# Shift and scale of two channel tiles by VectorE products along a channel's weights, and h by ScalarE

## The chip, the cores and the metric

The kernel runs on one core of one Trainium2 chip. The core has five engines, each with a queue of its own that is worked off in order: TensorE (PE in the profile, its weight loads PEld), VectorE (DVE), ScalarE (ACT), GpSimd (POOL) and SyncE (SP), which issues most of the DMA transfers. SBUF is the memory on the chip, with 128 partitions; PSUM holds what TensorE accumulates. The metric is the device time in microseconds (us) of one execution.

## What is computed

One layer of a backbone with two streams of 256 tokens each, context and latent, 2048 channels wide. Only this part of the reference is touched by the change:

```python
sc = jax.nn.silu(c)
scc = jax.nn.silu(c_ctx)
shift, scale, gate = jnp.split(sc @ w_ada[l] + b_ada[l], 3, axis=-1)
shift_c, scale_c, gate_c = jnp.split(scc @ w_ada[l] + b_ada[l], 3, axis=-1)
hc = _rmsnorm(ctx, g_pre[l]) * (1.0 + scale_c) + shift_c
zc = hc @ (w_in[l][:, :XBC_W + DT_W] if last else w_in[l])
hx = _rmsnorm(x, g_pre[l]) * (1.0 + scale[:, None]) + shift[:, None]
zx = hx @ w_in[l]
```

`_rmsnorm(x, g)` is x times 1/rms of its token, times g. After this follow a convolution, a bidirectional state-space scan, a spatial gating unit, an output projection and a last norm.

## The kernel before

The channels are cut into 16 tiles of 128, one channel on each partition, and the 512 tokens (context first, then latent) lie along the free dimension: `xT[:, k, :]` is channel tile k. h = x/rms * ha + hb is made tile by tile, where ha and hb are one number for each channel and stream. Products with `w_in` run in float32 split into two parts: a high part, rounded, and the low rest, so that each tile of outputs takes three matmuls (`mm3`: high by high, high by low, low by high). `hhi` and `hlo` are the two parts of h, `hi_st` and `lo_st` those of a weight row.

**The first stage** (to about 133.9 us) does three things at once.

1. *1/rms* (lines 260 to 282). Each of the 16 tiles is squared, by ScalarE and VectorE in turn, and summed over the partitions by matmuls with ones into `pss`. A transpose, a matmul with `sel` (`psb`), a square root, a reciprocal and another transpose give `rb`, 1/rms of each token on all partitions. A few warm-up matmuls (`warm`) lie in between.
2. *ha and hb* (`ada_mm`, `ada_fin`). The weights `w_ada` for shift and scale come in 32 chunks of 1 MB, two for each channel tile. Channel tiles 0 and 1 are a unit by themselves, the others form units of two: (2,3), (4,5) up to (14,15). A chunk of a pair holds a quarter of the input channels for its unit; `ada_mm` multiplies it by silu(c) and silu(c_ctx) (`sc`) on TensorE, 16 matmuls in float32, shown as 32 records, into `psada`. When a unit is complete, `ada_fin` transposes it on VectorE, and ScalarE makes ha and hb with two small activations for each tile.
3. *The rows* (line 372 on). Row kt takes weight row kt (`wst`, 480 KB, split by `split_st`: a cast on ScalarE, a small and a large subtraction on VectorE) and tile kt of h (`make_h`), and adds its share to `psdt` and to seven output tiles `psx`, two of which take latent tokens alone and are half as long. In `make_h`, VectorE multiplies x by ha and by rb, ScalarE adds hb and rounds (`hhi`), and VectorE takes the rest (`hlo`), each for the two streams apart.

The order on TensorE, VectorE, ScalarE and GpSimd is written by hand (`manual_schedule`): what `row_steps` lists for a row is issued in that order. ("m", i) stands for the products of output tile i (-1 is `psdt`), ("a", ci) for chunk ci, ("f", u) for `ada_fin`, ("h", k) for `make_h`, ("s", k) for `split_st`. From row 5 on a row is, in order, the split for the next row, two chunks, in odd rows the end of a unit, h for the next row, and its own eight products:

```python
return nxt[1:] + a + f + nxt[:1] + m
```

SyncE issues the loads in the order of the program: x in four transfers, then chunks and weight rows as line 372 on has them. A load waits until its buffer is free; there are six buffers for chunks (`raw0`) and three for weight rows (`st3`).

The last row (15) has an order of its own, `LAST`: `psdt`, tiles 4 and 5, each followed by a copy out of PSUM by VectorE (`zq`), then `dt_tok`, then the rest. `dt_tok` copies `psdt` by ScalarE and turns it by four matmuls against `fold` (`pstok`). `fold` is a small matrix made from the identity at line 165, at the start.

**The later stages** hold the convolution, the scan, the latent projections and the output projection. They have an order by hand up to the latent projections, and draw 121 weight tiles of 1 MB through four buffers that take the place of the first stage's. Later, `gate_tile` (line 884) forms the gate by another way than `ada_mm`: VectorE multiplies 2048 weights of a channel by c, laid out along the free dimension, and sums them in the same instruction (`accum_out`).

## Time and profile before

| | us |
|---|---|
| median of 3 runs | 995.4 (995.04 to 996.1) |
| the profiled execution | 995.27 |
| its span, first to last instruction | 993.6 |
| mean granted TensorE clock | 0.995 |

The profile is of one execution. Its page gives busy times of each engine and groups of instructions; other views of the same trace are the chain of work that ended last (followed back from the last instruction to what released each step), the timeline, the groups of a stretch, and a table of busy times by stretch.

How the page's slices and queues look:

```profile
PE   8999999999999999999999999999999999999996
PEld 3788887778787878787888888887888888888885
DVE  4345478877877665665667766666555554445636
ACT  4233348566656554545445434454565563346522
POOL 0000002423443221224000000000000000000000
PEclk9999999999999999999999999999999999999998
DMA  9999744233314324135888777774455445556722
```

Each digit is the busy share of one fortieth of the span (24.8 us) in tenths. The first stage fills a little over five of them: TensorE is near full there, VectorE at about a half, and the DMA engines are full for four slices. A group of instructions reads, for example, "L884 DVE SCALAR_TENSOR_TENSOR junk<-gate,cb 128x2048 bf16<-128x2048 f32 x16 | busy, mean ns of one | idle of the engine before them, and who released it": line, engine, operation, output and inputs, shape, count. Matmuls are pipelined: one has started its successor before its own modelled end, so the distance of two starts tells more than a duration.

### The profile page before, as it was taken

The page shows a single profiled execution, that of the slowest core. Times are in us where ns is not written, and L with a number is a line of the kernel's source. Part 1 is how long each engine was busy: PE and PEld are TensorE (multiplying, and loading weights), DVE is VectorE, ACT ScalarE, POOL GpSimd, SP SyncE. Part 2 cuts the span into 40 slices and gives each one's busy share as a digit, 9 for nine tenths or more (in the row PEclk, how much of TensorE's full clock was granted, in tenths as well). Part 3 has the DMA queues.
Part 4 walks back from the last instruction along what each step waited for, and adds up shares of the span by engine and source line. Part 5 has one row for each costly group of instructions (what it writes and reads, how often), then busy time and mean ns, then how long its engine had stood idle before and what let it go on. Part 6 is the DMA issues. An engine that isn't in the chain of part 4 may idle for free.

```text
span 993.6 us, 14183 instructions
## 1 busy us (share of the span) xinstructions
PE 976.9 (98%) x5636; PEld 791.0 (80%) x5636; DVE 622.6 (63%) x944; ACT 494.0 (50%) x759; POOL 112.3 (11%) x162
## 2 busy tenths in 40 slices
PE   8999999999999999999999999999999999999996
PEld 3788887778787878787888888887888888888885
DVE  4345478877877665665667766666555554445636
ACT  4233348566656554545445434454565563346522
POOL 0000002423443221224000000000000000000000
PEclk9999999999999999999999999999999999999998
DMA  9999744233314324135888777774455445556722
GB/s 379 419 417 419 300 179 170 85 128 128 128 43 170 127 85 158 54 138 203 301 306 294 280 263 291 266 284 171 170 173 204 174 169 212 181 200 235 274 85 84
DMA packets 31554, 207.28 MB, mean 209 GB/s; under 512 B 4080, under 2 KB 4208, under 8 KB 7808
## 3 DMA queue, kind: packets, MB, share of 16 engines
q1 hardware_dynamic: 28656, 192.52, 51.8%
q0 software_dynamic: 2112, 12.65, 3.7%
q10 hardware_dynamic: 720, 1.20, 0.3%
q8 instruction: 44, 0.72, 0.3%
q14 instruction: 22, 0.18, 0.1%
HBM read 204.20 MB, written 2.16 MB: 208 GB/s over the span
## 4 chain that ended last, share of the span: by engine, by line
PE 73%; issue 10%; DMA 9%; DVE 5%; ACT 1%; POOL 1%; SPq 0%; DVEq 0%; POOLq 0%; ACTq 0%
PE psx L138 10%; PE psx L140 10%; PE psx L139 10%; PE pa L1026 5%; PE pa L1028 5%; PE pa L1027 5%; DMA gate<-in_wada_dram 5%; PE pm L1075 3%; PE pm L1074 3%; PE pm L1073 3%; PE psada L215 3%; PE pq L1074 2%; PE pq L1075 2%; PE pq L1073 2%; DVE lo_w L82 2%
## 5 line engine op out<-in xcount | busy, mean ns | idle before, releaser
L82 DVE TENSOR_TENSOR lo_w<-w,hi_w 128x1024 fp32r<-128x1024 f32 x173 | 210.5, 1223 | 146.0 <-ACT hi_w L81 146.0
L81 ACT CAST hi_w<-w 128x1024 fp32r<-128x1024 f32 x173 | 182.0, 1052 | 202.3 <-PE pa L1028 130.4
L1026 PE MATMUL pa<-hi_w,hhi 128*128 128x512 f32 x512 | 202.4, 395 | 0.0
L1028 PE MATMUL pa<-hi_w,hlo 128*128 128x512 f32 x512 | 199.5, 390 | 0.0
L1027 PE MATMUL pa<-lo_w,hhi 128*128 128x512 f32 x512 | 199.3, 389 | 0.0
L138 PE MATMUL psx<-hhi,hi_w 128*128 128x512 f32 (+1 forms) x400 | 153.6, 384 | 0.0
L140 PE MATMUL psx<-hhi,lo_w 128*128 128x512 f32 (+1 forms) x400 | 145.9, 365 | 0.0
L139 PE MATMUL psx<-hlo,hi_w 128*128 128x512 f32 (+1 forms) x400 | 145.7, 364 | 0.0
L1026 PEld LDWEIGHTS pa<-hi_w,hhi 128*128 128x128 f32 x512 | 96.2, 188 | 20.6 <-issue 1.6
L1028 PEld LDWEIGHTS pa<-hi_w,hlo 128*128 128x128 f32 x512 | 96.1, 188 | 20.2
L1027 PEld LDWEIGHTS pa<-lo_w,hhi 128*128 128x128 f32 x512 | 96.2, 188 | 19.5 <-issue 0.2
L495 DVE SCALAR_TENSOR_TENSOR xbc<-psx,pc,xbc 128x248 f32<-128x248 f32 (+1 forms) x204 | 83.5, 472 | 34.1 <-ACT xbc L479 33.1
L420 DVE TENSOR_TENSOR lo_w<-w,hi_w 128x1024 fp32r<-128x1024 f32 x61 | 79.4, 1308 | 23.8 <-ACT hi_w L414 23.7
L138 PEld LDWEIGHTS psx<-hhi,hi_w 128*128 128x128 f32 x400 | 75.5, 189 | 13.4 <-issue 3.1
L140 PEld LDWEIGHTS psx<-hhi,lo_w 128*128 128x128 f32 x400 | 75.4, 189 | 12.6
L139 PEld LDWEIGHTS psx<-hlo,hi_w 128*128 128x128 f32 x400 | 75.6, 189 | 12.1 <-issue 1.7
L414 ACT CAST hi_w<-w 128x1024 fp32r<-128x1024 f32 x61 | 63.5, 1044 | 26.0 <-PE psx L139 12.9
L884 DVE SCALAR_TENSOR_TENSOR junk<-gate,cb 128x2048 bf16<-128x2048 f32 x16 | 36.6, 2290 | 22.8 <-DMA gate<-in_wada_dram 22.8
L1073 PE MATMUL pm<-hi_w,hhi 128*128 128x512 f32 x128 | 50.0, 390 | 0.0
L1074 PE MATMUL pm<-lo_w,hhi 128*128 128x512 f32 x128 | 49.9, 390 | 0.0
L1075 PE MATMUL pm<-hi_w,hlo 128*128 128x512 f32 x128 | 49.6, 389 | 0.0
L138 PE MATMUL psx<-hhi,hi_st 128*128 128x512 f32 (+1 forms) x112 | 41.3, 368 | 0.0
(219 smaller groups left out, 1324.3 us busy)
## 6 DMA issues: line engine op xcount, KB each, us to landing
w<-in_wlat_dram SPq DMA_DIRECT2D x64, 1024.0 KB, 4.8
ada<-in_wada_dram SPq DMA_DIRECT2D x32, 1024.0 KB, 14.7
w<-in_wout_dram SPq DMA_DIRECT2D x32, 1024.0 KB, 4.8
w<-in_wxbc_dram SPq DMA_DIRECT2D x25, 1024.0 KB, 4.8
gate<-in_wada_dram SPq DMA_DIRECT2D x16, 1024.0 KB, 5.8
R<-acs POOLq DMA_DIRECT2D x8, 1024.0 KB, 5.1
wst<-in_wst_dram SPq DMA_DIRECT2D x16, 480.0 KB, 14.9
xT<-in_xch_dram SPq DMA_DIRECT2D x4, 1024.0 KB, 8.0
```

The lines of the kernel that those rows point to most:

```text
L81: nc.scalar.copy(hi, raw)
L82: nc.vector.tensor_tensor(lo, raw, hi.bitcast(F32), op=ALU.subtract)
L138: nc.tensor.matmul(ps, lhsT=whi, rhs=hhi[k][:, s], start=start, stop=False)
L139: nc.tensor.matmul(ps, lhsT=whi, rhs=hlo[k][:, s], start=False, stop=False)
L140: nc.tensor.matmul(ps, lhsT=wlo, rhs=hhi[k][:, s], start=False, stop=stop)
L495: nc.vector.scalar_tensor_tensor(ao, zi, cw[:, k : k + 1], ao, op0=ALU.mult, op1=ALU.add)
L1026: nc.tensor.matmul(pa[tk], lhsT=hhi[k][:, t], rhs=whi[:, w], start=k == 0, stop=False)
L1027: nc.tensor.matmul(pa[tk], lhsT=hhi[k][:, t], rhs=wlo[:, w], start=False, stop=False)
L1028: nc.tensor.matmul(pa[tk], lhsT=hlo[k][:, t], rhs=whi[:, w], start=False, stop=k == KT - 1)
L1073: nc.tensor.matmul(p, lhsT=yh[:, t], rhs=whi[:, w], start=j == 0, stop=False)
L1074: nc.tensor.matmul(p, lhsT=yh[:, t], rhs=wlo[:, w], start=False, stop=False)
L1075: nc.tensor.matmul(p, lhsT=yl[:, t], rhs=whi[:, w], start=False, stop=hf == 0 and j == 15)
```

## The change

- **Tiles 12 and 13** no longer go through `ada_mm`. Their four chunks are laid out with 2048 weights of one output channel along the free dimension, one chunk for scale and one for shift of each tile, and `ada_v` multiplies such a chunk by silu(c) of one stream, laid out the same way on all partitions, and sums it, on VectorE. Two chunks and two streams make four products for a tile (`v12.0.0` to `v12.1.1`, `v13.0.0` to `v13.1.1`), eight in all. `ada_vfin` (step "e") then makes ha and hb as before. The unit (12,13) is gone.
- **silu(c) on all partitions** is made at the start: `c_diag` (VectorE) puts four times 128 values on diagonals, `c_rows` (TensorE) multiplies them by ones, `c_keep` (ScalarE) copies the result into `y`, which is free in the first stage. There are eight such blocks of 512. The warm-up matmuls fall from eight to three.
- **1/rms in front**: VectorE multiplies all of x by `rb` tile by tile (`norm`): tile 0 within the split of row 0, tiles 1 to 3 ahead of row 0, and tiles 4 to 15 in one block in row 0 (step "n").
- **h by ScalarE**: an activation with ha as scale and hb as bias makes h. For tiles 0 to 3 it writes `hhi` directly, and VectorE makes the unrounded h a second time for `hlo`. From tile 4 on it writes h in place for each stream, a copy rounds it, and VectorE takes the rest in one operation of 512 in place of two of 256.
- **The order**: the rows follow a table `WITH`, the loads a table `LOADS`. `load_more` issues loads in that order as far as buffers are free: four chunk buffers at first, since two of the six hold the squares and diagonals, and six after `make_h(0)`. Chunks that stood in pairs stand partly apart ("p3 a6.0 p2 a6.1 p3": three products, a chunk, two products, a chunk, three products).
- **`fold`** is made in `dt_tok`, in the last row, and `A` gets a place of its own, since `y` is now in use.

```diff
+UNITS = ((0,), (1,), (2, 3), (4, 5), (6, 7), (8, 9), (10, 11), (14, 15))
+VTILES = (12, 13)
+
+LOADS = "u0.0 w0 u0.1 u1.0 u1.1 w1 u2.0 u2.1 u2.2 u2.3 w2 w3 u3.0 u3.1 u3.2 u3.3 w4 w5 u4.0 u4.1 u4.2 u4.3 w6 w7 " \
+        "u5.0 u5.1 u5.2 u5.3 w8 w9 v12.0 v12.1 u6.0 u6.1 u6.2 u6.3 w10 w11 w12 v13.0 v13.1 u7.0 u7.1 u7.2 u7.3 w13 w14 w15"
+
+WITH = (
+    "p1 a1.0 p1 a1.1 p1 f1 h1 n p3 a2.0 p2 a2.1",
+    "p3 a2.2 p2 a2.3 f2 h2 s2 h3 p3",
+    "s3 p3 a3.0 p2 a3.1 p3",
+    "s4 p2 a3.2 a3.3 f3 h4 s5 h5 p6",
+    "p2 a4.0 a4.1 p6",
+    "s6 a4.2 a4.3 f4 h6 s7 h7 p8",
+    "p3 a5.0 p2 a5.1 p3",
+    "s8 a5.2 a5.3 f5 h8 s9 h9 v12.0.0 p8",
+    "v12.0.1 p3 a6.0 p2 a6.1 p3",
+    "v12.1.0 s10 p1 a6.2 p2 a6.3 f6 h10 v12.1.1 e12 h11 p5",
+    "s11 h12 v13.0.0 p8",
+    "v13.0.1 s12 v13.1.0 p3 a7.0 p2 a7.1 p3",
+    "s13 p1 a7.2 p2 a7.3 f7 v13.1.1 e13 h13 p5",
+    "s14 h14 p8",
+    "s15 h15 p8",
+    "",
+)
...
-    nc.vector.tensor_reduce(fold, ident.rearrange("p (g m) -> p m g", g=2), axis=mybir.AxisListType.X, op=ALU.add)
...
+    def ada_v(kt, c, v):
+        raw = ada_raw[f"v{kt}.{c}"]
+        nc.vector.scalar_tensor_tensor(junk, raw, 1.0, y[:, v, :], op0=ALU.mult, op1=ALU.mult,
+                                       accum_out=vsum[:, kt, c, v : v + 1])
+        if v == 1:
+            give("a")
...
+    def c_diag(*bs):
+        for b in bs:
+            v, k = b // 4, 4 * (b % 4)
+            nc.vector.tensor_tensor(dg4[:, b % 3].rearrange("p (k m) -> p k m", k=4), bc(ident, 1, 4),
+                                    bc(sc[:, k : k + 4, v], 2, P), op=ALU.mult)
+
+    def c_rows(*bs):
+        for b in bs:
+            cbp[b] = acp.tile([P, 512], F32, tag="acc", name=f"psr{b}")
+            nc.tensor.matmul(cbp[b], lhsT=ones, rhs=dg4[:, b % 3], start=True, stop=True)
+
+    def c_keep(*bs):
+        for b in bs:
+            nc.scalar.copy(y[:, b // 4, (b % 4) * 512 : (b % 4 + 1) * 512], cbp.pop(b))
+
     warm(2)
+    c_diag(0, 1)
+    c_rows(0, 1)
...
         if g == 3:
-            warm(1)
+            c_keep(*((0, 1), (2,), (3,), (4,))[k // 4])
+            c_diag(*((2, 3), (4, 5), (6,), (7,))[k // 4])
+            if k < 12:
+                c_rows(k // 4 + 2)
...
-    ada_mm(0)
-    ada_mm(1)
-    warm(2)
+    c_rows(5, 6)
+    ada_mm(0, 0)
+    ada_mm(0, 1)
+    c_rows(7)
+    warm(1)
...
+    def norm(*ks):
+        for k in ks:
+            nc.vector.tensor_tensor(xT[:, k, :], xT[:, k, :], rb, op=ALU.mult)
+
     def make_h(kt):
         sl = (slice(256, 512), slice(0, 256))
...
+        else:
+            full = x
+            for v, s in enumerate(sl):
+                nc.scalar.activation(x[:, s], x[:, s], AF.Identity, bias=hb[:, kt, v : v + 1], scale=ha[:, kt, v : v + 1])
+            nc.scalar.copy(hhi[kt], x)
+        nc.vector.tensor_tensor(hlo[kt], full, hhi[kt].bitcast(F32), op=ALU.subtract)
 
     def dt_tok():
+        nc.vector.tensor_reduce(fold, ident.rearrange("p (g m) -> p m g", g=2), axis=mybir.AxisListType.X, op=ALU.add)
         nc.scalar.copy(zdt, psdt)
...
-    sp0[0] = split_st(0)
+    split_st(0)
     ada_fin(0)
     make_h(0)
+    c_keep(7)
+    room["a"] += 2
+    load_more()
+    norm(1, 2, 3)
+    split_st(1)
```

More of the change, by code (lines that the diff above doesn't have):

```diff
@@ L183, in tile_hybrid_ssd_mlp, with load_more, give, ada_mm @@
     nc.vector.tensor_copy(sel[:, 1:4], bc(sel[:, 0], 1, 3))
-    ada_raw = {}
-    UNITS = [(0,), (1,)] + [(m, m + 1) for m in range(2, KT, 2)]
-    def ada_place(ci):
-        if ci < 4:
-            return ci // 2, 64, 8 * (ci % 2), 8
-        return ci // 4 + 1, 128, 4 * (ci % 4), 4
-    def ada_load(*cs):
-        for ci in cs:
-            ada_raw[ci] = load_raw(wada[ci], f"ada_{ci}")
+    ada_raw, wraw = {}, {}
+    todo = LOADS.split()
+    room = {"a": 4, "w": 3}
+    sq4, dg4 = (wp["raw"].tile([P, 4, 512], F32, tag="raw", name=n) for n in ("sq4", "dg4"))
+    def load_more():
+        while todo:
+            kind = "w" if todo[0][0] == "w" else "a"
+            if not room[kind]:
+                return
+            it = todo.pop(0)
+            room[kind] -= 1
+            if kind == "w":
+                kt = int(it[1:])
+                w = st3.tile([P, WST], F32, tag="wst", name=f"wst{kt}")
+                nc.sync.dma_start(w, wst[kt])
+                wraw[kt] = w
+            else:
+                u, n = (int(q) for q in it[1:].split("."))
+                row = 2 * UNITS[u][n // 2] + n % 2 if it[0] == "u" else 2 * u + n
+                ada_raw[it] = load_raw(wada[row], f"ada_{it[0]}{u}_{n}")
+    def give(kind):
+        room[kind] += 1
+        load_more()
     ada_ps = {}
-    def ada_mm(ci):
-        u, n, k0, nk = ada_place(ci)
-        if k0 == 0:
+    def ada_mm(u, c):
+        n = 64 * len(UNITS[u])
+        nk = 512 // n
+        if c == 0:
             ada_ps[u] = spt([P, 512], f"psada{u}")
         ps = ada_ps[u]
-        raw = ada_raw.pop(ci)
+        raw = ada_raw.pop(f"u{u}.{c}")
         for kk in range(nk):
-            k = k0 + kk
+            k = nk * c + kk
             for g in range(4):
@@ L354, in step @@
         elif what == "s":
-            sp0[i] = split_st(i)
+            split_st(i)
+        elif what == "v":
+            ada_v(i, *r)
+        elif what == "e":
+            ada_vfin(i)
+        elif what == "n":
+            norm(*range(4, KT))
         elif what == "z":
```

102 lines of the change are left out of this document (51 added, 51 removed).

## The prediction, made before the changed kernel ran

> **What bounds the kernel now.** I read the span, then a table of stretches cut at the stage borders, then the chain of work that ended last.
>
> ```profile
> span 993.6 us, 14183 instructions
> ```
> ```profile
> 23.20:62.00 38.80, 37.01 (x558) 28.80 (x559) 16.14 (x35) 11.65 (x25) 0.00 (x0) 1.00 1.01 418
> 62.00:133.90 71.90, 71.90 (x846) 60.50 (x845) 35.16 (x72) 28.88 (x57) 0.00 (x0) 1.00 0.86 352
> 133.90:300.00 166.10, 164.71 (x860) 132.67 (x859) 136.20 (x258) 105.10 (x188) 59.27 (x77) 1.00 0.33 118
> ```
> The columns of the table are PE, PEld, DVE, ACT and POOL, then clock, DMA share and GB/s. The first stage ends at about 133.9. TensorE is busy all through 62 to 133.9 and in 164.7 of the 166.1 us that follow; DMA is full only early (418 GB/s) and at a third afterwards. What TensorE saves or loses in the stage should therefore move the end one for one. The span is 993.6 us and its execution took 995.27, against a median of 995.4.
>
> ```profile
> 38.53 0.33 DVE adat L222
> 38.88 0.39 ACT ha L224
> ...
> 39.88 0.91 ACT hhi L310 x2
> 40.79 0.89 ACT hi_st L299
> 41.98 0.50 PE psdt L362
> ...
> 76.51 1.89 PE psada L215 x64
> ...
> 83.25 1.88 PE psada L215 x64
> ...
> 123.88 0.23 PE psdt L363
> 124.34 0.23 PE psx L139
> 128.50 0.23 PE psdt L363
> 130.10 0.84 PE pstok L320 x8
> ```
> This is the chain in the stage: start, duration, what. A later row is 83.25 - 76.51 = 6.74 us: two weight chunks (1.88) and its own products. Into row 2 the chain leaves TensorE: transpose, four small activations (38.88 to 39.88), h, the cast.
>
> ```profile
> 49.10 0.19 PEld L362 LDWEIGHTS psdt<-hhi,hi_st 128*128 128x128 f32 x1
> ```
> A row without chunks is 128.50 - 123.88 = 4.62, so a pair of chunks costs 6.74 - 4.62 = 2.1 in its row. The row just shown, from the timeline of weight loads, starts row 3: row 2, whose two chunks stand apart, takes 49.10 - 41.98 = 7.1.
>
> **The change, part by part.** Prices come from these groups (mean ns after the comma):
>
> ```profile
> L884 DVE SCALAR_TENSOR_TENSOR junk<-gate,cb 128x2048 bf16<-128x2048 f32 x16 | 36.6, 2290 | 22.8 <-DMA gate<-in_wada_dram 22.8
> ```
> ```profile
> L301 DVE TENSOR_TENSOR lo_st<-wst,hi_st 128x896 fp32r<-128x896 f32 x16 | 17.3, 1084 | 0.0
> ...
> L264 DVE TENSOR_TENSOR y<-xT 128x512 f32<-128x512 f32 x8 | 5.2, 689 | 6.4 <-DMA xT<-in_xch_dram 3.4 <-PE pss L268 3.0
> ```
> ```profile
> L224 ACT ACTIVATE ha<-adat,bsc,pc 128x2 f32<-128x2 f32 x16 | 6.1, 381 | 37.4 <-DVE adat L222 37.4
> L266 ACT ACTIVATE y<-xT 128x512 f32<-128x512 f32 x8 | 4.8, 626 | 4.1 <-DMA xT<-in_xch_dram 3.5 <-PE pss L268 0.5
> L226 ACT ACTIVATE hb<-adat,pc 128x2 f32<-128x2 f32 x16 | 4.5, 280 | 0.0
> ```
> *Removed.* The four chunks of tiles 12 and 13 leave TensorE: two pairs of 2.1, **-4.2 us**.
>
> *Products of the two tiles.* Eight products with sum of the L884 form, 2.29 each, 18.3 us on VectorE. Its load in the saturated stretch is 35.16 of 71.9, so there is room in total; what counts is the order. Three places follow; each begins at a matmul's end.
>
> Price of h from tile 4 on: two activations that now read a scale as well as a bias. Two with a bias took 0.91; reading the scale too costs 381 - 280 = 0.10 each (L224 against L226). With the copy of 512 elements (0.63 in L266's form, a little of it overlapped) I take 1.5 until hhi is there; hlo, like L264, takes 0.65 to 0.69 more, and the second matmul of the next row needs it 0.23 after the first.
>
> Row 10. After the last chunk of tiles 10 and 11 TensorE has five tiles left (p5): of 4.62 us, three full and two half tiles, 2.8. Transpose 0.35, four small activations 1.0, h 1.5: 2.9. Waits of 0.1 and, for hlo, 0.4: **+0.5**.
>
> Row 11. Behind hhi of tile 10 stand, in order: its hlo 0.65, the last product of tile 12 2.29, two small activations 0.5, h of tile 11 1.5, and, behind that on ScalarE, the cast for row 11 with the first subtraction (40.79 to 41.98, so 1.2): 6.15. TensorE has 0.4 + 4.62 = 5.0. **+1.2**.
>
> Row 13. From the last chunk of tiles 14 and 15: transpose 0.35, the last product of tile 13 2.29, small activations 0.5, h 1.5: 4.7 against p5's 2.8; 1.9 and hlo's 0.5: **+2.4**. It needs VectorE to arrive in time, and this is close: from hhi of tile 11 to that transpose it has two hlo, three splits of 1.3 (1.08 and a small first subtraction) and three products, 12.1 us, while TensorE takes 1.2 of waiting, 7.1 of row 11 and 4.4 of row 12: 12.7. Any surplus adds in full.
>
> The other six products would add 13.7 us without cover; what hides them is TensorE's rows 7 to 12.
>
> *Chunks apart.* Rows 6, 8, 9, 11 and 12 place their chunks apart, where they ran as pairs. Row 2 shows 7.1 against 6.74, of which a late lo is about 0.13: 0.2 each, five times, **+1.0** (bounds 0.5 and 1.9).
>
> *The start.*
>
> ```profile
> 18.00 1.10 PE L215 MATMUL psada<-ada,sc 128*32 128x64 f32 x64
> 19.77 1.10 PE L215 MATMUL psada<-ada,sc 128*32 128x64 f32 x64 [0.67 <-DMA ada<-in_wada_dram]
> 20.80 1.99 PE L256 MATMUL psw<-ones 128*128 128x512 f32 x4
> 23.21 0.50 PE L362 MATMUL psdt<-hhi,hi_st 128*128 128x512 f32 x1 [0.42 <-ACT hhi L310]
> ```
> Eight matmuls spread c over all partitions; four take the place of warm-up matmuls, two lie in the waits on the loads of x. Two stand ahead of the first chunks: 18.0 + 1.7 (two warm ones, 1.99 with their tail) + 2.2 = 21.9, where the warm-up behind the second chunk began at 20.8. The new h0 saves the two products ahead of hhi; transpose 0.3, activations 0.5, h 1.0 lead to 23.8 instead of 23.21: **+0.6** (0 if the second chunk still waits for its load and ends as before, 1.2 if nothing is saved).
>
> The eight diagonal products and ScalarE's eight copies lie in those same waits, but for ScalarE's last ones, behind h0. The products by 1/rms of tiles 4 to 15 are one block of 12 x 0.66 = 7.9 on VectorE in row 0, and the transpose for row 2 (due at 38.53, now 39.1) is queued behind it. Ahead of it stands tile 1, now behind the split of row 1, which waits for its load.
>
> ```profile
> ada<-in_wada_dram SPq DMA_DIRECT2D x7, 1024.0 KB, 17.4
> xT<-in_xch_dram SPq DMA_DIRECT2D x4, 1024.0 KB, 8.0
> wst<-in_wst_dram SPq DMA_DIRECT2D x2, 480.0 KB, 15.9
> ```
> (Issues of the first 20 us.) Eight loads of 1.05 MB (x and four chunks) and two of 0.49 take 22.5 us at 418 GB/s; with the first start and the last landing I put the second wst at 25 to 27, an estimate. Cast, subtraction, transpose, h1 and its hlo end between 29.8 and 31.8, the block between 37.7 and 39.7: 0 to 0.6 and the scale operands' 0.1, **+0.5**.
>
> *SyncE's queue.* The loads come in a new order of the same bytes. The last chunk is behind 36 loads of 1.05 MB and 13 of 0.49: 44 MB, at about 108 us and needed at about 115, 9.5 us into rows that begin near 105; this hides, with some 5 us to spare. The last wst waits for row 12's split, late on VectorE (about 112), and the next stage's weights are issued behind it; they are needed behind row 15, some 20 us later, with DMA at a third: 0.
>
> *fold.*
>
> ```profile
> 7.46 0.28 DVE L165 TENSOR_REDUCE y<-ident 128x64 f32<-128x128 f32 x1
> ```
> ```profile
> 129.46 1.37 DVE L357 COPY y<-psx 128x512 f32<-128x512 f32 x2 [4.27 <-PE psx L140]
> ```
> The reduction that made it early (L165) now stands in the last row, on VectorE behind two copies out of PSUM, and the pstok matmuls need it. The copies end at 129.46 + 1.37 = 130.83, plus 0.28 = 131.1, where pstok began at 130.1: **+1.0**. Both copies wait for TensorE's own products, so nothing hides this; behind pstok stand the rest of row 15 and the next stage.
>
> Sum: -4.2 + 0.5 + 1.2 + 2.4 + 1.0 + 0.6 + 0.5 + 1.0 = **+3.0**. On 995.27 that is 998.3; on the median 998.4.
>
> [...]
>
> ```profile
> 4.90:8.10 3.20, 1.18 (x9) 1.00 1.04 435
> 8.10:11.60 3.50, 3.50 (x9) 0.52 0.99 419
> 38.50:42.00 3.50, 1.92 (x10) 1.00 0.99 408
> ```
> Columns here: PE alone, clock, DMA, GB/s. After 1.18 busy of 3.2 us came a stretch at 0.52; after 1.92 of 3.5 the clock stayed (42 to 62 lies in the row with 1.00). Waits of 2.4 between matmuls are nearer the second row. [...]
>
> **The rivals.**
>
> *Hidden in part (22%).* The row waits turn out half as long and the early block ends in time: 2.0 + 0.5 less, +0.5: 995.9. For it: the starts of queued activations overlap by about 0.1. Against: the 2.29 stands in the chain whatever overlaps.
>
> *The written order is not the issue order (12%), the faster side.* If the planner moves fold and the products forward to where VectorE idles, rows 10, 11, 13 and fold lose their 5.1: -2.1, 993.3, and 992.2 if start and block are free too. It decides by where L165 runs: in the trace it ran at 7.46, behind products written a hundred lines later. But it stood ahead of the section whose order is by hand, and inside that section the last rows above come as written. [...]
>
> *Slots by strict turn (7%).* If the second chunk of tile 13 gets the slot of tile 12's second chunk instead of the first one free, its load waits for row 9's product (at about 101 instead of 92) and the five chunks behind it with it: the first chunk of row 11 comes about 5 us late, row 13 1.4 more: +9.4, 1004.8.
>
> *The clock falls in the waits (6%).* One stretch of 3.4 us at half clock behind row 13 costs 1.7: 1000.1.
>
> **How the numbers follow.** Forecast 53%, 997.5 to 1001.5. A measurement can tell about 0.2%, 2 us, from no change. Slower: 53 + 7 + 6 = 66%; within: 22%; faster: 12%. Low ends of start, block and gaps (0, 0, 0.5) and half the row waits (2.0) give -0.7; the high ends (1.2, 0.6, 1.9), with VectorE 1 us late at row 13, +5.6. The range 994.0 to 1001.5 takes these, the part-hidden and the clock case, and leaves out the faster case and the slots, 19%.
>
> **What would show it.** Right: psada with 128 matmul records fewer (one unit); TensorE idle for about 2 us ahead of psdt of row 13, released by ScalarE's hhi; about 1 ahead of row 11, by hi_st; pstok waiting for VectorE's reduction; pstok about 3 us later than 130.1. Wrong: no idle time in rows 10 to 13 (then the order or the price of a product), psada waiting for DMA (the loads), or a stage end that moved while the whole did not (the later stages absorb).

## The result, and the profile after

The changed kernel took 1003.58 us (median of 4 runs, 1001.63 to 1005.84) against 995.75 us: 1.0082 times the time before (95% interval 1.0070 to 1.0094), some 7.8 us more. The forecast of 998.4 had the sign right and the size wrong by 5 us. The profiled execution took 1001.63 us, 6.4 more than the one of before.

First the span from the page of the changed kernel, then its table of stretches, cut as before (PE, PEld, DVE, ACT, POOL, then clock, DMA share, GB/s):

```profile
span 999.9 us, 13966 instructions
```
```profile
23.20:62.00 38.80, 34.02 (x517) 25.80 (x521) 21.75 (x40) 14.06 (x28) 0.00 (x0) 1.00 0.96 396
62.00:133.90 71.90, 68.86 (x736) 54.50 (x727) 38.61 (x51) 30.91 (x60) 0.00 (x0) 1.00 0.89 363
```

TensorE, busy for 37.01 and 71.90 us of these stretches before, now has 34.02 and 68.86: it is idle 3 us more in each, and the DMA share of the first one fell from 1.01 to 0.96. What TensorE waited for in the stage (the view of waits from 23 us to the end of the stage: total, times, longest), first before, then after:

```profile
PE psdt L362 <- DVE hi_st L300: 1.6, 1, 1.6
PE psdt L362 <- ACT hhi L310: 0.4, 1, 0.4
PE psada L215 <- DMA ada<-in_wada_dram: 0.2, 1, 0.2
```
```profile
PE psada L256 <- DMA ada_u<-in_wada_dram: 2.6, 1, 2.6
PE psdt L449 <- DVE hi_st L371: 2.4, 2, 1.7
PE psdt L449 <- ACT hhi L399: 1.9, 2, 1.7
PE pstok L408 <- DVE y L404: 1.1, 1, 1.1
PE psdt L450 <- DVE hlo L400: 0.7, 3, 0.2
```

Three of the new waits are of the kind that the prediction named. The first, and largest, is not: a chunk of weights that had not landed. The timeline has the places (idle time of TensorE ahead of each in brackets):

```profile
33.08 1.08 PE L256 MATMUL psada<-ada_u,sc 128*32 128x128 f32 x32 [2.55 <-DMA ada_u<-in_wada_dram]
...
36.53 0.50 PE L449 MATMUL psdt<-hhi,hi_st 128*128 128x512 f32 x1
45.57 0.50 PE L449 MATMUL psdt<-hhi,hi_st 128*128 128x512 f32 x1 [1.71 <-DVE hi_st L371]
...
107.49 0.50 PE L449 MATMUL psdt<-hhi,hi_st 128*128 128x512 f32 x1 [0.69 <-DVE hi_st L371]
...
123.69 0.50 PE L449 MATMUL psdt<-hhi,hi_st 128*128 128x512 f32 x1 [1.74 <-ACT hhi L399]
...
136.58 1.08 PE L408 MATMUL pstok<-y 128*128 128x64 f32 x8 [1.07 <-DVE y L404]
```

These are the starts of rows 1, 2, 11 and 13 and of pstok. The 1.71 ahead of row 2 is not new: before shows 1.6 at the same place. Cut at the first psdt matmul of rows 0, 1, 5 and 15 and at pstok, the time lies as follows (us, from the timelines of the two profiled executions):

| stretch | before | after | difference |
|---|---|---|---|
| start to row 0 | 23.21 | 23.25 | 0.0 |
| row 0 to row 1 | 9.88 | 13.27 | +3.4 |
| row 1 to row 5 | 31.77 | 31.94 | +0.2 |
| row 5 to row 15 | 63.24 | 65.04 | +1.8 |
| row 15 to pstok | 1.84 | 3.07 | +1.2 |
| pstok to the end of the span | 863.7 | 863.3 | -0.4 |

The stage carries all of it, and behind it only 0.4 is given back. More than half of the loss lies in one row, for whose length the prediction had next to no term.

**Row 0.** SyncE's timeline of the changed kernel, where each line is a load issued:

```profile
8.88 2.78 SPq L229 DMA_DIRECT2D wst<-in_wst_dram  x2
13.74 0.33 SPq L466 DMA_DIRECT2D dtc<-in_dtp_dram  x1
16.24 0.33 SPq L467 DMA_DIRECT2D A<-in_dtp_dram  x1
17.41 0.33 SPq L468 DMA_DIRECT2D dsk<-in_dskip_dram  x1
19.95 7.91 SPq L101 DMA_DIRECT2D ada_u<-in_wada_dram  x4
```

Lines 466 to 468 are three small loads that stand in the loop at row 5, and before issued them there, at about 57 us. Here they go out at 13.7 to 17.4, ahead of the four chunks of unit 2. So does the second load of the first line, the weights of row 2, which stand behind unit 2 in `LOADS`. The order by hand covers TensorE, VectorE, ScalarE and GpSimd, in both kernels. SyncE is not in that list, so the order of its loads is the planner's; that they are issued in the order of the program held for the kernel before, and not for this one. The chunks of unit 2 were blocked, since two of their buffers still held squares of x (in experiment 1 they wait 7.0 us for the sums of these squares), and what was not blocked went ahead. What that does to the queue is in SyncE's own waits in the first 40 us, of the changed kernel and then of experiment 1:

```profile
SPq L467 <- DMA ada_u<-in_wada_dram: 2.2, 1, 2.2
SPq L466 <- DMA xT<-in_xch_dram: 2.1, 1, 2.1
SPq L101 <- DMA dtc<-in_dtp_dram: 1.2, 1, 1.2
```
```profile
SPq L101 <- PE pss L335: 7.0, 1, 7.0
```

In the changed kernel an issue waits until an earlier load has landed. Counted along the timeline it is the one eight places before (the four loads of x land one after the other, and the tenth to thirteenth issues follow at 6.4, 8.9, 11.3 and 13.7). Three of the eight places were held by loads of 32, 32 and 16 KB, and a chunk then waited for dtc to land. Meanwhile the transfers ran nearly dry. Two stretches of the changed kernel, and behind them the same two of the first experiment (DMA share and GB/s are the last columns):

```profile
26.00:28.00 2.00, 2.00 (x68) 1.50 (x69) 0.00 (x0) 0.93 (x1) 0.00 (x0) 1.00 0.36 117
28.00:30.00 2.00, 2.00 (x11) 1.68 (x11) 1.39 (x3) 0.55 (x3) 0.00 (x0) 1.00 0.78 310
```
```profile
26.00:28.00 2.00, 2.00 (x68) 1.49 (x69) 0.00 (x0) 0.65 (x1) 0.00 (x0) 1.00 0.99 413
28.00:30.00 2.00, 2.00 (x11) 1.70 (x11) 1.39 (x3) 0.55 (x2) 0.00 (x0) 1.00 1.06 430
```

Why they ran dry stays open. It was not for want of loads: the first two chunks of unit 2, issued at 19.95 and 22.41, were under way and landed at 32.95 and 35.5. From 26 to 28 us 260 of the 303 packets were smaller than 512 B, against 8 to 23 in each two us from 20 to 26; by that, most of them were those of the small loads. But in the kernel before the same three loads moved between 66 and 69 us with the DMA share at 1.03 to 1.06, so they do not slow the transfers wherever they stand.

**Row 13** went as forecast, on VectorE and ScalarE of the changed kernel:

```profile
119.03 0.32 DVE L283 STREAM_TRANSPOSE adat<-psada 128x128 f32<-128x128 f32 x1 [0.44 <-PE psada L256]
119.27 2.25 DVE L266 SCALAR_TENSOR_TENSOR junk<-ada_v,y 128x2048 bf16<-128x2048 f32 x1
...
121.57 0.29 ACT L274 ACTIVATE hb<-vsum,pc 128x2 f32<-128x2 f32 x1 [0.87 <-DVE junk L266]
121.90 1.09 ACT L398 ACTIVATE xT<-xT,hb,ha 128x256 f32<-128x256 f32 x2
123.02 0.62 ACT L399 CAST hhi<-xT 128x512 fp32r<-128x512 f32 x1
```

The last product of tile 13 stands between the transpose and h of tile 13, and TensorE starts row 13 when hhi is there, at 123.69. So did the end of the stage: the reduction for fold came behind the two copies out of PSUM, and pstok begins when it is done, at 136.58.

```profile
134.87 1.37 DVE L444 COPY y<-psx 128x512 f32<-128x512 f32 x2 [5.42 <-PE psx L166]
...
136.15 0.28 DVE L404 TENSOR_REDUCE y<-ident 128x64 f32<-128x128 f32 x1
```

### The profile page after: what moved, and what is told of

Its sections match the earlier page's. It is cut to its first block, busy times and chain, and to the rows that moved or that the text cites. A ratio compares the mean times of both kernels' runs of the same rounds, so it can differ in the third digit from the quotient of the medians.

```text
span 999.9 us, 13966 instructions
## 1 busy us (share of the span) xinstructions
PE 977.8 (98%) x5514; PEld 787.8 (79%) x5514; DVE 640.9 (64%) x944; ACT 507.2 (51%) x779; POOL 112.2 (11%) x162
## 4 chain that ended last, share of the span: by engine, by line
PE 91%; DMA 3%; DVE 2%; ACT 2%; issue 0%; SPq 0%; DVEq 0%; ACTq 0%
PE pa L1114 12%; PE pa L1116 12%; PE pa L1115 12%; PE psx L164 10%; PE psx L166 9%; PE psx L165 9%; DMA ada_u<-in_wada_dram 3%; PE pm L1163 3%; PE pm L1162 3%; PE pm L1161 3%; PE psada L256 2%; PE pq L1163 2%; PE pq L1162 2%; PE pq L1161 2%; PE psc L785 1%; PE pso L838 1%
## 5 line engine op out<-in xcount | busy, mean ns | idle before, releaser
L164 PEld LDWEIGHTS psx<-hhi,hi_w 128*128 128x128 f32 x400 | 75.5, 189 | 13.5 <-issue 3.1
L972 DVE SCALAR_TENSOR_TENSOR junk<-gate,cb 128x2048 bf16<-128x2048 f32 x16 | 36.7, 2291 | 24.1 <-DMA gate<-in_wada_dram 24.1
```

Of the source, the lines that this page charges most:

```text
L164: nc.tensor.matmul(ps, lhsT=whi, rhs=hhi[k][:, s], start=start, stop=False)
```

## The experiments

The theory behind the first four: the loss is in separate pieces, namely the loads (2.5), fold (1.2), and the order of the products in rows 10 to 13. The main rival: the sum on record was right and something outside the stage, or in the clock, makes the rest. All times are medians; before was 995.6 to 996.0 beside each group.

**1. SyncE in the written order**

```diff
-    man.enter_context(tc.manual_schedule(engines={ET.PE, ET.DVE, ET.Activation, ET.Pool}))
+    man.enter_context(tc.manual_schedule(engines={ET.PE, ET.DVE, ET.Activation, ET.Pool, ET.SP}))
```

> Theory (loads): by row 1 the changed kernel is 3.5 us behind the kernel before because SyncE issues the second-row weights and three small loads ahead of the first chunk of unit 2, against the written order. With SyncE's order by hand as well, TensorE's wait of 2.6 us for that chunk goes, row 2 begins near 42.5 to 43 instead of 45.6, pstok near 133.5 instead of 136.5, and the whole falls by about 3 us, to 998 to 999. Rival (start): the loss comes from the matmuls that spread c and from VectorE's block of products, and the loads only cover it: row 2 stays at 45 or later and the whole within 1 us of the changed kernel.

Measured: 1001.09 us, 1.0060 (1.0042 to 1.0078): 2.5 less than the change, where about 3 was expected. The first chunk of unit 2 lands at 29.8 instead of 32.95 us. The wait on the load is gone from the view of TensorE's waits, row 0 to row 1 takes 11.15 instead of 13.27, and the DMA share stays at one (the two rows shown above). The loads cost 2.1 to 2.5 us, the three small ones and the weights of row 2 together, since this edit puts both back. The profiled execution gave more than half of it back: from 122.8 to 126.2 its clock was at one half (the long matmuls start 0.43 us apart there instead of 0.23, and the mean clock from 100 to 137 us is 0.95), and rows 5 to 15 took 66.63 instead of 65.04. That was the first sign of the clock.

**2. The three small loads by GpSimd's queue**

```diff
-            nc.sync.dma_start(dtc, dtp[0:1].partition_broadcast(P))
-            nc.sync.dma_start(A, dtp[1:2].partition_broadcast(P))
-            nc.sync.dma_start(dsk, dskip.partition_broadcast(P))
+            nc.gpsimd.dma_start(dtc, dtp[0:1].partition_broadcast(P))
+            nc.gpsimd.dma_start(A, dtp[1:2].partition_broadcast(P))
+            nc.gpsimd.dma_start(dsk, dskip.partition_broadcast(P))
```

> The three small loads (dt bias, a_log, d_skip) go by GpSimd's queue; the weights of row 2 still stand ahead of unit 2's first chunk. Theory (loads): the DMA gap at 26 to 30 us and the three landings go, which gives back about 2.3 of the 3.5 us, and 1.2 stay for the weights of row 2: row 2 begins near 43.3. Rival (start): nothing comes back. A second rival within the theory (weights of row 2 alone): only 0 to 0.6 comes back.

Measured: 1004.01 us, 1.0089 (1.0073 to 1.0105), no gain in total, where 2.3 was expected, but the pieces tell more: row 0 to row 1 takes 11.06, and the wait on the chunk is gone, although the planner still orders the rest and the weights of row 2 still go ahead of unit 2. What was won there is lost at the start. GpSimd has nothing to wait for and issues them at 2.7 to 4.2 us, among the loads of x. From issue to landing, the loads of x took (min, median, max), in the changed kernel and in this run:

```profile
DMA to landing us min/median/max: 5.1/8.1/11.1
```
```profile
DMA to landing us min/median/max: 5.1/10.9/14.0
```

Row 0 begins at 26.17 instead of 23.25. The chunk lands at 32.6 here, hardly earlier than the 32.95 of the changed kernel; the wait is gone because the row that needs it begins 2.9 later. Counted from the landing of the last load of x (16.6 us here, 13.7 in the changed kernel, 13.5 in experiment 1) the chunk comes 16.0 us later, against 19.2 and 16.3. So the three small loads cost about 3 us in both places, ahead of x or ahead of unit 2, and no cost of the weights of row 2 shows beside them.

**3. fold at the head of the last row**

```diff
     def dt_tok():
-        nc.vector.tensor_reduce(fold, ident.rearrange("p (g m) -> p m g", g=2), axis=mybir.AxisListType.X, op=ALU.add)
...
+        if kt == KT - 1:
+            nc.vector.tensor_reduce(fold, ident.rearrange("p (g m) -> p m g", g=2), axis=mybir.AxisListType.X, op=ALU.add)
```

> The reduction that makes fold stands at the head of the last row's VectorE work instead of behind the two copies. Theory (order on VectorE): TensorE's wait of 1.1 us ahead of pstok goes and the whole falls by 1.0 to 1.1 us. Rival (next late): ScalarE's copy of psdt or tile 5's products end as late, and pstok gains less than 0.4.

Measured: 1002.66 us, 1.0074 (1.0055 to 1.0092). Row 15 to pstok takes 1.84, exactly as before the change, against 3.07: fold cost 1.2. The profiled execution ended its span at 998.8, 1.1 below the changed kernel's.

**4. Another order of the products**

```diff
-    "s8 a5.2 a5.3 f5 h8 s9 h9 v12.0.0 p8",
-    "v12.0.1 p3 a6.0 p2 a6.1 p3",
-    "v12.1.0 s10 p1 a6.2 p2 a6.3 f6 h10 v12.1.1 e12 h11 p5",
+    "s8 a5.2 a5.3 f5 h8 s9 h9 v12.0.0 v12.0.1 p8",
+    "v12.1.0 v12.1.1 e12 p3 a6.0 p2 a6.1 p3",
+    "s10 p1 a6.2 p2 a6.3 f6 h10 h11 p5",
     "s11 h12 v13.0.0 p8",
-    "v13.0.1 s12 v13.1.0 p3 a7.0 p2 a7.1 p3",
-    "s13 p1 a7.2 p2 a7.3 f7 v13.1.1 e13 h13 p5",
+    "s12 v13.0.1 v13.1.0 p3 a7.0 p2 a7.1 p3",
+    "s13 v13.1.1 e13 h13 p1 a7.2 p2 a7.3 f7 p5",
```

(A letter stands for a step: s split, a chunk, f end of a unit, h, v product, e small activations of a VectorE tile, p products of the row.)

> The products of tiles 12 and 13 are moved forward: tile 12's last one ahead of row 8's chunks, tile 13's last one ahead of row 12's chunks, so that none stands between the end of a unit and the h that follows. Theory (order of the products): the waits ahead of rows 11 and 13 (1.7 to 1.9 each, and 0.5 for hlo) go for the most part and pstok comes 3 to 4 us earlier. Rival (VectorE's load): eight products of 2.29 us do not fit, the waits turn up ahead of rows 9 to 12 on hi_st or lo_st, and pstok gains less than 1.5 us.

Measured: 1003.89 us, 1.0086 (1.0070 to 1.0102): no change in the median. The waits ahead of rows 11 and 13 are gone, and one of 2.1 us stands ahead of row 10. Rows 5 to 15 took 64.89 with a stretch at half clock among them (105.0 to 108.4, clock 0.50), behind that wait; by what such a stretch costs in experiments 1 and 8, 1.2 to 1.6, they would have been about 1.5 shorter without it and 1.6 below the changed kernel's, half of the 3 to 4 that the theory had. A second such stretch lies in row 0 (33.3 to 36.7, clock 0.50). So the order may be worth that much in its rows; the total does not show it.

**5. Loads, fold, order and the block of 1/rms together**

```diff
-    "p1 a1.0 p1 a1.1 p1 f1 h1 n p3 a2.0 p2 a2.1",
+    "p1 a1.0 p1 a1.1 p1 f1 h1 p3 a2.0 p2 a2.1",
...
-    "s3 p3 a3.0 p2 a3.1 p3",
+    "s3 n p3 a3.0 p2 a3.1 p3",
...
+    "s8 a5.2 a5.3 f5 h8 s9 h9 v12.0.0 v12.0.1 p8",
+    "v12.1.0 p3 a6.0 p2 a6.1 p3",
+    "s10 p1 a6.2 p2 a6.3 f6 h10 h11 p5",
+    "s11 v12.1.1 e12 h12 p8",
+    "s12 v13.0.0 v13.0.1 p3 a7.0 p2 a7.1 p3",
+    "s13 v13.1.0 v13.1.1 e13 h13 p1 a7.2 p2 a7.3 f7 p5",
```

with the edits of experiments 1 and 3 (n is the block of products by 1/rms).

> Four edits on the changed kernel at once: SyncE's loads in the written order, the reduction for fold at the head of the last row, the block of products by 1/rms moved from row 0 to row 2 (behind its split), and the products of tiles 12 and 13 regrouped so that a split is never queued behind the last product of a tile. Theory (four separate terms, each seen in the changed kernel's trace): loads -2.3, fold -1.1, the 1.71 us that TensorE waits ahead of psdt of row 2 by hi_st -1.5, the waits ahead of rows 10, 11 and 13 (0.16, 0.69, 1.7 and hlo's 0.4) -2.5. From the changed kernel without half-clock stretches, 1002.0: about 994.6; with fewer waits also fewer half-clock stretches. Rival (the waits only move: VectorE's 18.3 us of products have no room in these rows): rows 10 to 13 keep their 3 us, 997.1. Rival (the time is in the chunks apart and the clock): nearer 1000.

Measured: 1001.47 us, 1.0059 (1.0045 to 1.0073); the first theory missed by 7. Two of its steps fell. The wait ahead of row 2 stayed at 1.7 with the block moved away, and the move cost 1.3 in rows 1 to 5, 0.8 of it a new wait ahead of row 4: the block had not been in the chain. And four products between row 10 and row 13 are more than VectorE has room for: it works from 110.4 to 120.7 without a gap, and TensorE waits for what comes behind (a stretch at half clock follows, 124.8 to 128.2; the mean clock from 100 to 137 us is 0.95):

```profile
122.88 0.49 PE L448 MATMUL psdt<-hhi,hi_st 128*128 128x512 f32 x1 [3.13 <-ACT hhi L399]
```

**6. Tiles 12 and 13 back on TensorE**, all the rest of the change as it is

```diff
-UNITS = ((0,), (1,), (2, 3), (4, 5), (6, 7), (8, 9), (10, 11), (14, 15))
-VTILES = (12, 13)
+UNITS = ((0,), (1,), (2, 3), (4, 5), (6, 7), (8, 9), (10, 11), (12, 13), (14, 15))
+VTILES = ()
...
+    "s9 a6.0 a6.1 h9 p8",
+    "s10 a6.2 a6.3 f6 h10 p8",
```

and rows 6, 7 and 10 to 13 likewise, with the loads in the order of the units.

> The changed kernel with tiles 12 and 13 back on TensorE as a ninth unit, and rows 6 to 14 with their chunks in pairs as before the change; all the rest (c spread over the partitions and kept, h by ScalarE, 1/rms in front, the planner's order of loads, fold late) stays. Theory of the sum on record: the shift's own terms were -4.2 + 0.5 + 1.2 + 2.4 + 1.0 = +0.9, so undoing them gives -0.9: 1002.7 against the median of 1003.6. By the rows of the trace (rows 5 to 15 take 65.0 us changed, 63.2 before): -1.8, 1001.8, or 1000.2 without half-clock stretches. Rival (the shift itself gains, the rest of the edit costs): slower than 1004. If the loads, the block and fold carry the rest of the loss, 4 to 6 us above before remain.

Measured: 1001.05 us, 1.0050 (1.0038 to 1.0063): 2.4 less than the changed kernel beside it (1003.46). Rows 5 to 15 take 63.24, to the hundredth what they took before. The shift as the change has it therefore costs 1.8 on the path, where the sum on record had 0.9. And 5 us of the loss have nothing to do with it.

**7. The long waits filled with matmuls**

```diff
+        elif what == "k":
...
+                nc.tensor.matmul(ada_ps[i], lhsT=ones, rhs=ones[:, 0:1].to_broadcast([P, 512]), start=True, stop=True)
```

four of them ahead of the late chunk of row 0, three ahead of row 2, one ahead of row 11, three ahead of row 13.

> The changed kernel with warm matmuls (results unused) in TensorE's four longest waits: four ahead of the chunk of row 0 that waits for its load, three ahead of row 2, one ahead of row 11, three ahead of row 13; nothing else. Theory (the changed kernel's runs, 1001.6 to 1005.8, fall into two groups because a wait now and then brings on stretches of 3.41 us at half clock, 1.7 us each): with the waits filled every run has a mean granted clock of 0.997 or 0.998, the runs lie within 1.5 us, the median is 1002.0 to 1002.6. Rival (the spread has another cause): two groups as before, median about 1003.6.

Measured: 1003.24 us, 1.0074 (1.0061 to 1.0087). All five runs had a mean clock of 0.997, and they lie between 1002.94 and 1004.26. The median came 0.6 above what was expected, because the filling itself cost: row 0 to row 1 takes 14.31, 1.0 more than in the profile of the changed kernel, and rows 1 to 5 take 32.45, 0.5 more.

**8. The changed kernel once more**

> The changed kernel once more, for its spread and a profile. Theory (half-clock stretches): the runs with a mean granted clock of 0.997 or more take 1001.6 to 1002.5, those of 0.993 to 0.994 take 1004.5 to 1006; where the profile has half-clock stretches in the first stage, each follows a wait of TensorE and lengthens its row by about 1.7 us. Rival: time and clock do not go together.

Measured: 1003.46 us (1002.40 to 1005.25). With the first four runs there are nine of this kernel. The four with a mean clock of 0.997 or 0.998 took 1001.63, 1002.40, 1002.41 and 1003.46; the two at 0.995 took 1003.20 and 1003.63; the three at 0.993 and 0.994 took 1004.75, 1005.25 and 1005.84. This profile has two stretches at half clock in the stage. Four consecutive pieces of it, a stretch and the one ahead of it (PE, PEld, DVE, ACT, POOL, clock, DMA share, GB/s):

```profile
29.87:33.28 3.41, 1.06 (x16) 0.62 (x18) 2.78 (x6) 1.30 (x4) 0.00 (x0) 1.00 1.02 423
33.28:36.70 3.42, 3.42 (x37) 2.66 (x26) 3.42 (x7) 0.00 (x0) 0.00 (x0) 0.50 1.02 426
122.05:125.46 3.41, 1.67 (x8) 1.05 (x6) 1.27 (x3) 2.52 (x5) 0.00 (x0) 1.00 0.96 368
125.46:128.87 3.41, 3.18 (x8) 2.48 (x8) 2.59 (x6) 3.38 (x7) 0.00 (x0) 0.50 1.00 413
```

The first follows the wait on the load, the second the wait ahead of row 13. Row 0 to row 1 takes 14.46 here against 13.27, rows 5 to 15 take 66.50 against 65.04: 1.2 and 1.5 for a stretch, where the theory had 1.7. Experiments 7 and 8 together: the waits bring on the half clock, in some runs and not in others, and that is most of what spreads the changed kernel's runs over 4 us. Not all of it: the run of 1003.46 with a clock of 0.998 is outside the theory's range, and the runs of before spread from 994.9 to 998.1 without following the clock.

**9. Tiles on TensorE, and loads, fold and row 0's chunks put right**

To experiment 6 the edits of 1 and 3, and in row 0

```diff
-    "p1 a1.0 p1 a1.1 p1 f1 h1 n p3 a2.0 p2 a2.1",
+    "p1 a1.0 p1 a1.1 p1 f1 h1 n p5 a2.0 a2.1",
```

> The run with tiles 12 and 13 back on TensorE (median 1001.05), and with it three edits: SyncE's loads in the written order, fold's reduction at the head of the last row, and the two chunks of unit 2 in row 0 side by side as before the change. Theory (the loads cost 2.3 to 2.5, fold 1.1, the chunks apart in row 0 about 0.4, and with the long wait on a load its half-clock stretch goes): 1001.05 - 2.4 - 1.1 - 0.4 = 997.1, down to 996.4 without the half-clock stretches; row 1 at about 33.8, pstok at about 131.5. Rival (what is left above before, 5 us, is somewhere else, in the later stages or in c's spread): 999 or more.

Measured: 996.01 us, 1.0003 (0.9994 to 1.0013): the time of before. Row 0 to row 1 takes 10.56, row 15 to pstok 1.84. So c spread over the partitions, h by ScalarE and 1/rms in front, which all stay, cost no more than the total can show; in the pieces of this one profile they come to 1.2 (0.4 at the start, 0.7 in row 0, 0.2 in rows 1 to 5). The loss was the loads, fold, the chunks of row 0, the shift, and the clock.

**10. The three edits on the changed kernel, with its shift as it is**

> The changed kernel with the three edits alone (SyncE's loads in the written order, fold's reduction at the head of the last row, unit 2's chunks in row 0 side by side), the shift of tiles 12 and 13 and the order of its products as the change has them. Theory (in the changed kernel the shift costs 1.8 us on rows 5 to 15, 65.0 against 63.2, beyond the 0.9 of the sum on record, and its 1.7 us wait ahead of row 13 brings on a half-clock stretch in some runs): 1.8 above the same kernel with the tiles on TensorE (996.0), so 997.8, up to 999.5 in runs with such a stretch. Rival (the three edits do not add up: what they give back is lost in the shift's waits): 1000 or more.

Measured: 999.19 us, 1.0031 (1.0019 to 1.0044); two of six runs at 997.4 and 997.5. That is 4.3 below the changed kernel for the three edits, and 3.2 above experiment 9: 1.8 for the shift by the rows (rows 5 to 15 take 65.07), the rest probably half clock in the other four runs, which took 999.19 to 1000.44 at a mean clock of 0.995 or 0.996, against 0.997 for the two. Its profile has one such stretch, at 43.9 (clock 0.50 to 47.3). That one follows a wait of 2.1 ahead of row 2 and not one of the shift's, so the 3.2 are not all the shift's.

**11. The shift with its products regrouped**, and the three edits

```diff
+    "s8 a5.2 a5.3 f5 v12.0.0 h8 s9 h9 v12.0.1 p8",
+    "v12.1.0 v12.1.1 p3 a6.0 p2 a6.1 p3",
+    "s10 p1 a6.2 p2 a6.3 f6 h10 h11 e12 p5",
+    "s11 h12 v13.0.0 p8",
+    "s12 v13.0.1 v13.1.0 p3 a7.0 p2 a7.1 p3",
+    "s13 v13.1.1 e13 h13 p1 a7.2 p2 a7.3 f7 p5",
```

> The shift on VectorE kept, with the same three edits, and its eight products regrouped: the first of tile 12 between the transpose for tile 8 and the hlo of tile 8, where VectorE was idle 2.7 us in the run with the other order; tile 12's small activations behind h of tile 11; the last of tile 13 ahead of row 12's chunks. Theory (the shift's cost was only the order of its products on VectorE, of which the other order kept 2.1 us in row 10): rows 5 to 15 take 61 to 61.5 us against 65.0 and 63.2 before, 1002.0 - 2.3 - 1.1 - 0.4 - 3.7 = 994.5; that is 2 below the run with the tiles on TensorE that stands beside it. Rival (VectorE has no room: a wait of 2 to 3 us comes back in row 10, 12 or 13, as it did in the first regrouping): 996.5 to 998, no better than the tiles on TensorE.

Measured: 996.52 us, 1.0007 (0.9998 to 1.0015). The rival was nearer: rows 5 to 15 take 63.60, no better than with the tiles on TensorE. What was late is one load ahead of row 13, in the timeline of this run:

```profile
112.81 1.00 ACT L370 CAST hi_st<-wst 128x960 fp32r<-128x960 f32 x1 [8.67 <-DMA wst<-in_wst_dram]
...
119.44 0.49 PE L448 MATMUL psdt<-hhi,hi_st 128*128 128x512 f32 x1 [1.32 <-ACT hhi L399]
```

The split of row 13, queued on VectorE ahead of tile 13's last product, waited for wst13.

**12. The same with wst13 ahead of unit 7's last chunks**

```diff
-u7.0 u7.1 u7.2 u7.3 w13 w14 w15
+u7.0 u7.1 w13 u7.2 u7.3 w14 w15
```

> The regrouped version (996.5) with one load moved: wst13 ahead of the last two chunks of unit 7 instead of behind them. In the regrouped run its split began at 112.8, when it landed, and TensorE waited 1.3 ahead of row 13 behind it. Theory: it lands 5 us earlier, that wait and hlo's 0.2 go: 995.1, within measurement of before. Rival (VectorE's own queue ends no earlier, the two last products of tile 13 stand in it anyway): 996.5, no change; or unit 7's last chunk comes late and row 12 waits for its load.

Measured: 995.55 us, 0.9996 (0.9987 to 1.0004): within the noise of before, not a gain that can be claimed. The rows did follow:

```profile
107.60 0.99 ACT L370 CAST hi_st<-wst 128x960 fp32r<-128x960 f32 x1 [3.62 <-DMA wst<-in_wst_dram]
...
117.80 0.40 PE L448 MATMUL psdt<-hhi,hi_st 128*128 128x512 f32 x1
```

Rows 5 to 15 take 61.54, 1.7 less than before, and the profiled execution's span is 992.2 against 993.6. Its eleven runs fall apart into five at 993.8 to 994.4 and six at 995.5 to 997.1; a wait of 2.0 ahead of row 2 remains. Their mean clocks (0.996 to 0.998 and 0.995 to 0.997) overlap, so what parts the two groups stays open.

The pieces of the stage side by side (us; h marks a stretch at half clock inside):

| kernel | start to row 0 | 0 to 1 | 1 to 5 | 5 to 15 | 15 to pstok | median |
|---|---|---|---|---|---|---|
| before | 23.21 h | 9.88 | 31.77 | 63.24 | 1.84 | 995.75 |
| changed | 23.25 | 13.27 | 31.94 | 65.04 | 3.07 | 1003.58 |
| 1 loads as written | 23.03 | 11.15 | 31.92 | 66.63 h | 3.07 | 1001.09 |
| 3 fold early | 23.04 | 13.70 | 31.92 | 65.05 | 1.84 | 1002.66 |
| 6 tiles on TensorE | 23.48 | 14.24 h | 31.89 | 63.24 | 3.07 | 1001.05 |
| 10 three edits | 23.21 | 10.30 | 33.87 h | 65.07 | 1.84 | 999.19 |
| 9 three edits, tiles on TensorE | 23.62 | 10.56 | 31.92 | 63.24 | 1.84 | 996.01 |
| 11 three edits, regrouped | 23.29 | 10.28 | 32.10 | 63.60 | 1.84 | 996.52 |
| 12 and wst13 earlier | 23.09 | 10.18 | 32.25 | 61.54 | 1.84 | 995.55 |

But for the clock and some tenths at the start, in row 0 and in rows 1 to 5 (see the block below), each column moves with its own edit and with no other. That is why the pieces can be added.

## Why the prediction missed

**The step that failed** is the one on SyncE's queue: "The loads come in a new order of the same bytes", this hides, 0. It worked out when the last chunk would land, at the far end of the stage, and took the written order for the order of issue. It had raised the question elsewhere (the rival in which the written order is not the issue order) but only for VectorE's products, which are under the order by hand. SyncE is not: the planner sent three small loads and the weights of row 2 ahead of unit 2, near the start of the stage, and the three small loads never came up in the prediction. Where it had 0 the runs show 2.1 to 2.5 us (experiment 1), lost in row 0, and experiment 2 puts them down to the three small loads. "psada waiting for DMA (the loads)" stood in the list of what would prove it wrong, and that is what the trace shows.

**The clock in the waits** was a rival at 6%, of one stretch in row 13 at 1.7. It was right in kind: a stretch cost 1.2 to 1.6 (experiments 1 and 8). Five of nine runs had a mean clock of 0.995 or less, and the median lies 1.1 above that of the four without and 1.8 above the profiled one. Here the prediction weighed the waits of 2.4 against one row of before (1.92 busy of 3.5, clock kept) and took them as safe. That was too coarse: in the profiles here the half clock followed stretches of 3.41 us with 0.70 to 1.67 of TensorE busy, so a wait of 2.4 inside one was not safe, and the largest wait came from a place that it had not foreseen.

**The other terms**, as forecast and as measured:

| term | forecast | measured |
|---|---|---|
| shift, rows 5 to 15 (chunks, waits of rows 10, 11, 13, chunks apart) | +0.9 | +1.8 |
| start | +0.6 | 0.0 |
| block ahead of row 2 | +0.5 | +0.1 |
| fold | +1.0 | +1.2 |
| loads | 0 | +2.1 to 2.5 |
| rest of row 0 | 0 | +0.9 to 1.3 |
| half clock, in the median | 0 | +1.1 to 1.8 |

The four terms that were not put at 0 came to 3.1 against the 3.0 of the forecast, but only by luck: the shift cost 0.9 more, and start and block cost 1.0 less.

*Shift.* The waits are where they were put: 0.16 and 0.22 for row 10 (0.5 forecast), 0.69 for row 11 (1.2), 1.74 and 0.22 for row 13 (2.4): 3.0 instead of 4.1. VectorE's product was priced well, 2.28 against 2.29. What was too small is the rest: 65.04 - 63.24 + 4.2 - 3.0 leaves 3.0 for chunks placed apart and for starting again after a wait, where 1.0 was forecast with an upper bound of 1.9. The rows tell the two apart. In experiment 12, rows 8, 11 and 12, each with one pair apart and next to no wait, take 7.05, 7.05 and 7.07, where a row with a pair takes 6.73 before: 0.3 for a pair, 1.6 for the five, which is above the forecast and within its bounds. The other 1.4 comes with the waits, and the prediction had no term for it: row 10 of the changed kernel has no chunks and takes 6.05, of which 0.69 and 0.22 are waits, and the 5.14 that are left compare with 4.61 before.

*Start.* Row 0 begins at 23.25 as it did at 23.21. The sum had the second chunk end at 21.9; it ended at 21.1, against 20.8 before, because what stands ahead of it came earlier (`psb` at 17.02 instead of 17.68). In the profile of the changed kernel the clock is full from 3.9 us on, where before had 8.2 to 11.6 at half; from 4.80 to 8.21, with the early spread of c, TensorE is busy for 3.0 us there, against 1.39 before. Whether the spread took the half clock away was not tried, nor whether row 0 would have begun later with it. The runs of before beside the experiments rather speak against such a cost of the half clock: the eleven with a mean clock of 0.995, that of the profile with this stretch, have a median of 995.1, and the sixteen with 0.998 one of 995.6.

*Block.* In the changed kernel the transpose for row 2 was not delayed: 1.71 against 1.58 of waiting, and experiment 5 moved the block without moving that wait. But there the late chunk hid the block. It ends at 39.2, and the transpose comes at 42.0 behind TensorE. In experiments 10 to 12, with the chunk in time, the transpose follows the block without a gap (in experiment 10 at 39.4), and the wait ahead of row 2 is 2.1, 1.9 and 2.0 against 1.7: 0.2 to 0.4, much as forecast.

*fold.* 1.2, and all of it came back in experiment 3. The forecast's 1.0 was reckoned from 130.1, where the chain has pstok; the timeline has it begin at 129.94.

*Rest of row 0.* Experiment 1 still took 11.15 against 9.88 there, and 10.30 with unit 2's chunks side by side (experiment 10). The chunks apart in row 0 cost 0.8; the prediction counted rows 6, 8, 9, 11 and 12 and passed over row 0. For the last 0.4, the timeline of experiment 10 shows a wait of 0.22 for hlo ahead of the second matmul and a gap of 0.32 inside the first chunk of unit 1, whose cause it does not show; before has neither.

Sum of the pieces of the first table: 0.0 + 3.4 + 0.2 + 1.8 + 1.2 - 0.4 is 6.2 of the profiled 6.4 us, and the half clock adds what the median has beyond that.

## What to carry to other kernels

Where only some queues are ordered by hand, look up the issue order of the others before costing them at nothing, the small loads first: three loads of 16 to 32 KB ahead of a large one cost 2 to 3 us here. A shift of work to an idle engine is worth what is left after its new waits, and here those ate it; the same shift gained 1.7 us in its rows only when each product stood where that engine was idle and its load was early, and the total does not show even that. Add up a stage by its pieces, since edits in different rows add, and look at the clock of every run before taking a difference of 2 us for an effect.

## What the runs showed of the hardware

*Half clock after a partly idle stretch.* In the trace of before the clock is full from 4.80 us for 3.41 us, at half from 8.21 for another 3.41, and full from 11.62 for 976.21 us, 286 times as long; in that of the changed kernel it is full from 3.94 for 989.86 us, 290 times as long. Counted in stretches of that length from 4.80, before has one up to 140 us with less than 1.8 us of TensorE busy: 1.39, followed by the one at half clock. The next, with 1.83, was followed by full clock. Counted from 3.94, the changed kernel has 1.57 as its least there, and no stretch at half clock. In the profiles of the experiments the stretches of 3.4 us ahead of half clock had 0.70 and 1.33 busy (experiment 4), 1.06 and 1.67 (8) and 1.26 (10). So 1.57 kept the clock and 1.67 did not: the busy time alone does not tell these two apart. The two waits of experiment 8's rows, in the profile of the changed kernel that kept its clock, in the same columns:

```profile
31.24:34.65 3.41, 1.57 (x34) 1.33 (x35) 3.40 (x6) 0.00 (x0) 0.00 (x0) 1.00 1.00 420
...
119.98:123.40 3.42, 1.97 (x11) 1.50 (x10) 1.55 (x2) 2.49 (x7) 0.00 (x0) 1.00 0.97 343
```

There each wait fell across the border of two such stretches, in experiment 8 into one.

*Eight loads under way.* In the changed kernel SyncE's issues, from the tenth at 6.4 us up to the chunk at 30.22, each go out 0.01 to 0.09 us after the landing of the load eight places before, large or small (that chunk when dtc had landed, 16.4 us after dtc's own issue). Whether the limit lies in the program or in the queue was not tried, nor whether it has a part in the two us at a DMA share of 0.36.

*Small loads can be dear.* The same 80 KB, issued by GpSimd's queue among the loads of x, made the last of these land 14.0 instead of 11.1 us after its issue (experiment 2). In the kernel before they moved at 66 to 69 us beside other loads, with 407 to 414 GB/s, and show no cost.
